# One ScalarE exponential over a two-bank PSUM tile for the first key tile of every head pair, with five single banks beside it

## The chip, the cores and the metric

The kernel runs on one core of a Trainium2 chip. The metric is the device time of one launch in microseconds (us); lower is better. Before the change the median of three runs is 174.76 us (173.38 to 174.87).

## The reference

Thresholded attention over 8 batches, 12 heads, 512 positions and 64 dimensions, in fp32:

```
scores  = einsum('bhqd,bhkd->bhqk', Q, K) / sqrt(64)
weights = softmax(scores)                      # over the keys
weights = where(weights > threshold, weights, 0)   # threshold 0.1
weights = weights / (sum(weights) + 1e-10)
out     = einsum('bhqk,bhkd->bhqd', weights, V)
```

Few weights of a softmax over 512 random scores pass 0.1, so most rows of the output are zero. The kernel uses that.

## The kernel before, in words

The 96 heads are taken as 48 pairs (hp), and two pairs make a quad (q, 24 of them). For each quad SyncE's queue loads Q and K. GpSimd casts Q to f16 (qcast, L371), TensorE transposes K in fp32 (ktr, L381) and Q in f16 (qtr, L410), ScalarE or VectorE copies the transposed K out of PSUM (kev, L389 and L391), VectorE the transposed Q (qev, L416), and GpSimd casts K to f16 (kh, L400). Squares of both for a bound on the norms (bits) are made by GpSimd (L425), VectorE (L429) or ScalarE (L427), and small matmuls (norms, L478) add them up.

Each pair has four key tiles t = 0 to 3. A step sc (L438) makes the scores of one key tile for both heads, two matmuls into two PSUM banks of 128 x 512 fp32. A step ex (L447 on ScalarE as a true exponential, L449 on VectorE as an approximation by the bits of an f16) reads one such bank and writes one half of an e tile. A step sm (L468) takes the e tile in four matmuls with a column of weights, and accumulates into one bank (sum) a row for each head, which later tells whether any query row of this pair can have a weight over the threshold. Three groups of 24, 16 and 8 pairs are closed one after the other (y, d, fl, mx), and for the few candidate rows the scores are computed again exactly (gq gathers the rows of Q, then xm, xev, xqk, xexp, xcut, xkeep), the row of V is gathered (gv) and scattered to the output (scatter), which 24 zero fills (z, L607) have blanked before.

PSUM has eight banks: seven in the pool `one`, one for `sum`. The pool `one` serves the scores, both transposes (two banks for each), the exact stage, the spare and warm-up matmuls, and one bank that the norms hold for most of the time.

What sets the order of all this is a table written out, ORDER: 1326 words, each of them a step's number in base 36 and a letter for the engine that does it (P TensorE, V VectorE, A ScalarE, G GpSimd, S and Q the DMA queues of SyncE and ScalarE, N none). The kernel issues the steps in that order, so every engine works through its own steps in the order of the table. A step that takes a buffer gets the one that came free first, and waits in place until it is free. The prices in `add(...)`, such as 0.478 us for an ex on ScalarE and 0.6 on VectorE, are those of the planner that such a table comes from; they do nothing at run time.

Of the kernel before, what the change touches and what calls it, by code (L numbers as in the profile page):

```python
# [9 lines left out]

ORDER = """6N fS 1G gS 7P hS 8P 5V 18S 24S 9P 22S aP 23S bP 16S 17Q 2vS iV jP 2tS nP kV lA cP mA oV 2uS dP pV 3qS qP yP rA sV eP 3pS zA 25V 10V 26P 19G uP 27A 12P 28V 3G wA 14V vA 1aP 29V 2aP 1bA 52S 2bV 1eP 1cA tP 2cV 13A xP 2wV 2dP 1fV 1dG 31P 1gV 2hP 2eA 32V 15P 1xG 2fV 2jA 2xP 33V 1tP 2yA 1pP 2zA 1vV 1uA 1hP 2iA 1jV 30G 2lP 1qA 11P 53S 2nV 3kG 3gP 1iA 2kP 6fS 1rV 1wP 2mA 38P 3iV 3hA 34P 36A 35V 3tP 3rG 3aA 1lP 3sG 3uV 3vA 37P 6gS 1nA 1mV 3yP 3wG 2pP 39A 7sS 3zV 3cP 2rA 40V 1sP 3lV 3dA 41P 2qV 56P 3mN 3xG 3eA 57A 58V 49P 2oP 4bA 54G 43V 45P 42A 3bP 55G 46V 4lP 47A 4tP 1yG 95S 4aV 4mA 44P 4dP 4vA 4nV 5bP 4uA 1kP 6jP 4eA 59G 5cV 5dV 1zN 2gP 6kA 6lV 5aG 5qP 4fV 5mP 5rA 6hG 5uP 1oP 5oA 5vV 6iG 7tS 5eP 5wA 5gV 6mG 96S 6oP 5fA 4oP 6pV 5sA aiS 5iP 6qV 4gP 5nA 5kV 7wP 5jA 6vP 7nV 7xA 4pP 7yV 6nG 4cP 6wA 5pP 6xV 6zP 7zG 4qA bvS 5yP 71V 70A 7oG 5tP 5hP 60A 4rV 7fP 99P 7gA 5zV 7jP 9aA 5xP 7kV 3jP 7hA 2sP 7uG 77P 9bA 66P 7vG 79V 78A 61P 5lP 9cG 67V 7lA 81P 7bP 9dG 68A 82V 7iP 6yP 7cA 97G 83V 6rP ajS 7dV 88P 98G 6tA 8cP bwS 89V 6sA 7mP 80G 3fP d8S 8aA 8eV 9eP 4xG 8dA amP 9fV 73P 9gV anA 7eP aoV 7pN 69P 74A a5P 8kP apG 75A a7V elS 62P a6A 4yG 4wP 8lV 84P 64A 7aP 86V 72P 85A 76P 8mA 63V 4hP 8gP 4iA 48P 4zN 8iV akG 9lP 8hA 9pP 4jV alG 9mA 8fP 87P 9rV 0G 9qA 8oP 8sP 9nA 8pV arP aqG 8tA 65P asV ioS a9P 8uA bxG atV a8P 8nP abA aaV byG auP 8qA 9hP 6aG avV b6P 9iA acP 8jP b7V 9jA 4kP b2P d9S awV b8A dcP b4A emS b3V a1P bqG ddA 8vP a3V k2S 9xP deA bzP a2V fzS 9zA ayP 9yV c0A fyS 9sP dfG biP azA c1V 8rP 8bP bkA bjV c4P c2G b0A 9tP 4sP c5V dgG 9vA 8wP 9uV baP c3G 8xA hcS a4P c6V axP bcA 8yV cfP epP chA bbV daG cbP eqA 9wP cgV dbG hbS b1P erA beP cdV 6bG 9oP bfA cjP bgV dhP ccA 9kP diV ckA czP clV cvP d0A bhP brG 6cN djV ciP cxA 8zP d1V ecP cwA dkP eeV bmP edA ceP b9P boA bnV bdP esG bsN dlA doP dmV crP enG dpA cmP dqV cnP eoG ctA e4P coV csA efP lfS etG 6uP blP e6A cpV g0G ipS euP e5A dsP adG evV e8P 21S dtA cyP ewV drP 3oS duA e9V g2P eaA exP g3V fdP g4A cqP feA cuP ezV g5G bpP eyA flP ffV g1G f5P fmA dnP fnV ebP aeG f7A k1S g7P f1P f6A g8V a0P e7P f3A g9V f9P f2A c7P fbV giP 2G afN c9A f0P foP 90V gkA dvP 51S faV fgP g6G gjA fhP c8V isP 91G fiA hfP fjV itA dwP iuA hgV f4P f8P dxA b5P dyV gqP k3G hhA 92N phS h2P gsV gaP grA k4G dzP gbA fcP gcV hdG d2P h3A fpP h4V heG geP fqA gdP ggV 4G gtP gfA gmP frV hkP goA guP leS hiG hlV ghP gvA fsP hmV glP iqG gnA gyP gwV hnP irG h0A e0P hpV gxP hjG hoA caP gzV gpP e2A ivG ixP i7P e1A iwG iyV hzP ekS i8A h5P izV lgG h1P i0V e3P i9A fkP lhG i1A j8P xtV hvP o4S j9A j4P 20P xuV j5A 6dP 7qP hxA btP xvN xwV 3nP agP j6A k5P xxV jaA jcP hwA o5S hqP xyV jdV jeA xzP msS 93P k6A 50P y0V ydV i3P mrS y1V k7A xrV y2G ibP i5A iaP i4V hyP idA ifP k8G icV joP ihA yeP ijG j7P yfV jfP igA jpV hrP 6eS ygV kaP htA jqV liP tlS hsA kbV jgP ljA h6V yhG huP kcV i2P jiA iiP lkV jhA jkP ikG khP jlV jsP kiA y3P jtV kjA klP egA y4V j0P knV k9G y5P ilN kmA h7V ehA juV h8N ysV j1V j2A ktP eiN llG piS yiP jmA kvV d3G tkS l1P yjA kpP y6A l3V ykP kqA y7V kuV krA mtG y8V l2A muG s7S lnP ylA kxP lmG loV mvP kyA ymV lpV d4G koP mwA ynV ksP l4P kzA meP mxV m2P mfA m6P mgV kkP m3A jnP s8S myG d5N m7V lyP m8A o8P jwG haS m0A m4V n0P lzA quS l0P n1V jbP o9A oaV kdP maP kfA n2V jrP o6G m5P mcV mbA n3P o7G n7P keA n5V mdP mzG m1P n8A qvS n4V nbP n9A mmG plP d7S ncV ndA ytP lqP fxS pmA pnV jvP n6P lrA nnP yuV lsV nvP noA pjG m9P yvV neP npV nwA obG l5P buS odP nxA l7V pkG miP l6A ieP oeV jxG luP mkA mjV ldS nqP j3P lvA ofV 7rS pqP lwA nrP yaV ogP 94S ntA mhP naP poG prV psV jyN ohA ltP oiV osP ocG nsA ptP ypV otV ooP ouA ywG l8P kgP oqV opA qyP puA pvV ppG q1P qzA uxS lxP s9G r0V pwP q2A p0P saG q3V owP p2A okP qwG oxV mlP oyA orP r1G p8P p1V omA sbP qxG olA paV qdP mqS ftG p9A ojP nuP scA sdV onP i6P qeV qfA q5P nfP uyS q6A q7V qlP yxP qnA seG nhV ngA r2G p4P yyV o3S r3P p5A p6V mnG pxP qmA p3P r4V kwP pzA q9P r5V pgS sgP qaA qbV qgP q8P pyA shV sfG riP moN njP yoV rjA rkV r6P nzG ovP nlA siV p7P nyP y9V r7A fuV ryP srP s0A yzP ssA ybG rzV r8A fvN stA nkV tmG jjP z0A tfV waS reP rqP tnG rgV toP rfA rsA yqG z1V r9P tpV nmP tqA q4P z2V t3P rrA rmP trG pbP t5A inS rnV o0G ttP roA rtP s6S z4V tuV ruP t4A qhP tvV wbS rvA qoP qiV ozP rwA twP uwS qjV t7P uzG o1N tyA k0S rpP t9V tsG u4P txA raP qtS usG u6A u5V rlP s1P rcA uoP t8V v1P rbA upV qcP uqA u8P z3V v2A v3V sjP ycG tjS q0P u9A rhP uaV ahS szP slA v0G weP skV t0A utG u0P wfV wgA niP qkP u1A rdP t1V rxP u2A snP z7V v6P soA ugP v4G v7V spA z8V ucP v5G uhA svP v8V z9N z5G ueA smP sxV sqP uiA vxP zaV v9P w9S swA t6P u3P vbA vaV wcG u7P udA w1P vyV wdG vtP vzA suP whG w2V ujP vuA ufP ubP s2G w3V vvA vpP wjP zbV vrA vdP taP vqA vfV tzP vwP veA wkV vlP wiG ukP vnA wlV vcP uuN s3G w0P umV ulA vhP wuP vmV vjA tbP t2P wvV wwA voP unP viA vsP tcV s4N wmP xmS tdA x2P zcV x6P wnA x3V vgP wxP woA urP x8V x4A wyP wqP x7V zdP wzA syP x5P zrV wsA vkP zeV x0V wrA xaP zgG xeP xcV xbA teP w4P xgA x1P xfV xdP wtP zfV x9P xiV xhP wpP zsP 106A ztV zhP w5V zvG 107V d6P ziA zjP 108N 109V 10aV 10bV tgV 10cP zkA zwP thN 10dV w6A 10fG h9P zxV zuV pcV zyP l9A w7N 10rV xjV z6G zlV xkN zmV znV zoV 10gP zzA zpG uvP 100V 10hA xlP qpV 101V 10iP yrG 102V laV pdV lbN peN zqG xnP 10jA xoP ejP qqA imP 10kV o2P 10lV tiP 104G mpP qrN xpP 10mV 10sV qsP 103V 10eV pfP 10nV fwP 10oG jzP xqP s5P w8P lcP 105G xsV 10qV 10tV 10pG"""


class Plan:
# [78 lines left out]
def kernel(  # L95
# [18 lines left out]
    nc = tc.nc  # L114
    B, H, S, D = Q.shape
    P = 128
# [26 lines left out]
    f32 = mybir.dt.float32  # L143
# [130 lines left out]
    nc.vector.memset(small[:], -SMALL)  # L274


    pools = {"one": 7, "sum": 1, "big": 32, "qh": 2, "e": 14,
             "y": 1, "vals": NG, "m": 2, "ix": NX, "qs": NX, "xq": 2, "cut": NX, "vr": NX}
    one = [psum.tile([P, S], f32, name=f"one{i}") for i in range(pools["one"])]
    sum_b = [psum.tile([P, S], f32, name=f"sum{i}") for i in range(pools["sum"])]  # L280

    def bufs(name, shape, dt):
# [33 lines left out]
    def at(pool, key):  # L316
        return plan.held[pool, key]
# [115 lines left out]
    def do_sc(eng, hp, t):  # L433
        q, n = divmod(hp, 2)
        qk = qk_b[big("qk", q)]
        for h in range(2):
            ps = slice(h * D, (h + 1) * D)
            nc.tensor.matmul(one[at("one", ("sc", hp, t, h))][:], lhsT=qk[ps, 1, n, t * P:(t + 1) * P], rhs=qk[ps, 0, n, :],  # L438
                             start=True, stop=True)

    kind = {}

    def do_ex(eng, hp, t, h):
        src = one[at("one", ("sc", hp, t, h))][:]
        dst = e_b[at("e", (hp, t))][:, h, :]
        if eng == "ACT":
            nc.scalar.activation(dst, src, ACTF.Exp, scale=scale, bias=-11.0 * math.log(2.0))  # L447
        else:
            nc.vector.tensor_scalar(dst.bitcast(u16), src, scale * LOG2E * 1024.0, 4096.0,  # L449
                                    op0=ALU.mult, op1=ALU.add)  # L450
        kind[hp, t, h] = 0 if eng == "ACT" else 1

    begun = set()

# [170 lines left out]
    for u in units:  # L625
# [39 lines left out]
        for hp in range(2 * q + n0, 2 * q + n0 + k):  # L665
            n = hp % 2
            for t in range(SO):
                g = 4 * hp + t
                add(("sc", hp, t), {"PE": 0.22}, 0.23, [("qev", u, 0), ("qev", u, 1), ("kh", q, n)], g - 3,
                    lambda e, hp=hp, t=t: do_sc(e, hp, t), takes=[("one", ("sc", hp, t, h)) for h in range(2)] + [("e", (hp, t))], mode="h")  # L670
                for h in range(2):
                    add(("ex", hp, t, h), {"ACT": 0.478, "DVE": 0.6}, 0.15, [("sc", hp, t)], g,
                        lambda e, hp=hp, t=t, h=h: do_ex(e, hp, t, h),
                        gives=[("one", ("sc", hp, t, h))])
                gr = group_of[hp]
                head = hp == first_of[gr] and t == 0
                add(("sm", hp, t), {"PE": 0.22}, 0.23,
                    [("ex", hp, t, 0), ("ex", hp, t, 1)] + ([("sm", first_of[gr], 0)] if not head else []), g + 2,
                    lambda e, hp=hp, t=t, gr=gr: do_sm(e, hp, t), takes=[("sum", gr)] if head else [],
                    gives=[("e", (hp, t))], mode="c")  # L680
        if not last:
# [172 lines left out]
```

## Time and profile before

| | |
|---|---|
| median of three runs | 174.76 us |
| the profiled execution | 173.97 us |
| its span, first to last instruction | 172.1 us |
| granted TensorE clock, mean | 0.992 |
| busy: PE, DVE, ACT, POOL | 159.3, 150.6, 146.7, 133.7 us |
| moved by DMA | 38.27 MB, mean 222 GB/s |

The profile is of one execution. The span is 1.9 us shorter than that execution's time, and that execution is 0.8 us below the median. Busy counts the union of an engine's instructions; instructions of one engine overlap at their ends, so the time from one start to the next is shorter than what one took. PE is matmul, PEld weight load, DVE VectorE, ACT ScalarE, POOL GpSimd, SP SyncE. L447 is line 447 of the kernel.

### The profile page before, as it was taken

Reading aid. Unit: us, or ns where it says so; the run is one execution under the profiler, and the core shown is the slowest. Engines: PE = TensorE matmul, PEld = TensorE weight load, DVE = VectorE, ACT = ScalarE, POOL = GpSimd, SP = SyncE. Lnnn points to the kernel's source line nnn. Section 1 sums busy time; section 2 is a strip of 40 time slices with the busy share of each in tenths; the row PEclk is TensorE's granted clock in tenths of the full one; section 3 lists DMA queues with packets and bytes.
Section 4 is the critical chain, followed back from the end, with each engine's and each line's share of the span. In section 5 each row is a group of like instructions: output and inputs, shape, how many; then the busy total and the mean of one; then the engine's idle time right before and its main releaser. Section 6 shows DMA issues by size and latency. Waiting matters only on the chain.

```text
span 172.1 us, 5805 instructions
## 1 busy us (share of the span) xinstructions
PE 159.3 (93%) x2190; PEld 62.5 (36%) x2190; DVE 150.6 (88%) x353; ACT 146.7 (85%) x294; POOL 133.7 (78%) x201
## 2 busy tenths in 40 slices
PE   5699999999999999999989999989999999999940
PEld 1253544342444234334432443434324333432410
DVE  5398999899999989989999899999999999989630
ACT  2279999999999999999899999999999999746300
POOL 5049794999988979993796999999899985226762
PEclk9999999999999999999999999999999999999996
DMA  4999998959899999878999996999999980000000
GB/s 103 290 281 175 268 255 224 265 132 313 183 244 304 277 229 339 242 181 251 276 280 289 221 272 156 365 409 311 318 304 338 415 344 13 2 3 8 3 3 9
DMA packets 67453, 38.27 MB, mean 222 GB/s; under 512 B 51941, under 2 KB 64349, under 8 KB 67424
## 3 DMA queue, kind: packets, MB, share of 16 engines
q1 hardware_dynamic: 66320, 37.63, 77.7%
q8 instruction: 17, 0.28, 0.7%
q0 software_dynamic: 576, 0.13, 0.5%
q10 hardware_dynamic: 528, 0.13, 0.3%
q14 instruction: 12, 0.10, 0.3%
HBM read 25.56 MB, written 12.78 MB: 223 GB/s over the span
## 4 chain that ended last, share of the span: by engine, by line
PE 55%; DMA 15%; DVE 10%; POOL 6%; ACT 4%; issue 4%; SPq 2%; POOLq 0%; DVEq 0%
PE one L438 20%; PE sum L468 19%; DMA qs<-in_Q_dram,idx 7%; PE one L556 6%; PE one L381 4%; PE one L410 3%; ACT e L447 3%; DMA out_dram<-zero 3%; POOL big L425 2%; DMA big<-in_K_dram 2%; DVE e L449 2%; DMA big<-in_Q_dram 2%; POOL qh L371 2%; PE one L541 2%; SPq L330 2%
## 5 line engine op out<-in xcount | busy, mean ns | idle before, releaser
L447 ACT ACTIVATE e<-one 128x512 f16<-128x512 f32 x238 | 123.3, 638 | 3.0 <-PE one L438 2.5
L449 DVE TENSOR_SCALAR e<-one 128x512 uint16<-128x512 f32 x146 | 93.5, 682 | 4.2 <-PE one L438 3.4
L438 PE MATMUL one<-big 64*128 64x512 f16 x384 | 66.4, 385 | 0.3
L468 PE MATMUL sum<-e,w_s 128*32 128x512 f16 (+1 forms) x768 | 58.4, 385 | 0.3 <-DVE y L495 0.2
L425 POOL TENSOR_TENSOR big<-big 128x512 bf16<-128x512 f16 x56 | 56.9, 1037 | 0.0
L400 POOL CAST big<-big 128x512 f16<-128x512 f32 x46 | 27.6, 611 | 8.6 <-DVE big L429 3.3
L371 POOL CAST qh<-big 128x512 f16<-128x512 f32 x45 | 26.5, 612 | 7.9 <-DVE qh L369 6.3
L438 PEld LDWEIGHTS <-big 64*128 64x128 f16 x384 | 17.1, 95 | 36.5 <-issue 28.0
L468 PEld LDWEIGHTS <-w_s 128*32 128x32 f16 (+1 forms) x768 | 15.3, 95 | 31.6 <-issue 27.0
L389 ACT COPY big<-one 128x512 f32<-128x512 f32 (+1 forms) x33 | 18.5, 591 | 3.8 <-PE one L381 3.8
L416 DVE COPY big<-one 128x512 f16<-128x512 f16 (+1 forms) x52 | 19.2, 396 | 1.2 <-PE one L410 0.7
L381 PE MATMUL one<-identity_f,big 64*128 64x64 f32 x384 | 18.1, 231 | 1.6 <-DMA big<-in_K_dram 1.4
L381 PEld LDWEIGHTS one<-identity_f,big 64*128 64x128 f32 x384 | 16.5, 143 | 6.4 <-issue 2.7
L534 POOL DMA_INDIRECT qs<-in_Q_dram,idx x6 | 6.4, 1072 | 12.5 <-DVE idx L524 12.2
L391 DVE COPY big<-one 128x512 f32<-128x512 f32 (+1 forms) x19 | 12.5, 657 | 1.3 <-PE one L381 0.6
L556 PE MATMUL one<-big,xq 128*32 128x512 f32 x96 | 11.5, 598 | 0.4 <-DVE xq L549 0.2
L410 PE MATMUL one<-identity_h,qh 64*128 64x64 f16 x384 | 10.8, 193 | 0.7 <-DVE qh L369 0.4
L410 PEld LDWEIGHTS <-qh 64*128 64x128 f16 x384 | 8.7, 96 | 7.2 <-issue 3.1
L600 POOL DMA_INDIRECT out_dram<-vr,idx x6 | 6.4, 1065 | 2.6 <-issue 1.1
L585 POOL DMA_INDIRECT vr<-in_V_dram,idx x6 | 6.4, 1060 | 2.3 <-DVE cut L566 1.2
L562 ACT ACTIVATE one<-one 128x512 f32<-128x512 f32 x6 | 3.5, 584 | 5.4 <-PE one L556 5.3
L429 DVE TENSOR_SCALAR big<-big 128x512 int32<-128x512 int32 x15 | 7.3, 491 | 0.1
(85 smaller groups left out, 80.8 us busy)
## 6 DMA issues: line engine op xcount, KB each, us to landing
out_dram<-zero SPq DMA_DIRECT2D x24, 512.0 KB, 6.9
big<-in_K_dram SPq DMA_DIRECT2D x95, 128.0 KB, 4.7
big<-in_Q_dram SPq DMA_DIRECT2D x22, 512.0 KB, 5.7
big<-in_Q_dram SPq DMA_DIRECT2D x4, 256.0 KB, 3.8
big<-in_K_dram ACTq DMA_DIRECT2D x1, 128.0 KB, 2.8
qs<-in_Q_dram,idx POOLq DMA_INDIRECT x6, 3.4
vr<-in_V_dram,idx POOLq DMA_INDIRECT x6, 2.4
out_dram<-vr,idx POOLq DMA_INDIRECT x6, 2.2
```

The source lines that it names most:

```text
L371: behind(nc.gpsimd.tensor_copy(dst, src))
L381: nc.tensor.matmul(dst[i][:, c:c + D], lhsT=src[ps, n0 + n, r, :], rhs=identity_f32[ps, ps], is_transpose=True, start=True, stop=True)
L389: nc.scalar.copy(dst, src)
L400: behind(nc.gpsimd.tensor_copy(dst, src))
L410: nc.tensor.matmul(dst[i][:, c:c + D], lhsT=src[ps, n0 + n, r, :], rhs=identity_h[ps, ps], is_transpose=True, start=True, stop=True)
L416: nc.vector.tensor_copy(qk_b[big("qk", q)][:, 0, n0:n0 + k, i * SO * D:(i + 1) * SO * D], src)
L425: behind(nc.gpsimd.tensor_tensor(out=dst[:, n, :], in0=src[:, n, :], in1=src[:, n, :], op=ALU.mult))
L438: nc.tensor.matmul(one[at("one", ("sc", hp, t, h))][:], lhsT=qk[ps, 1, n, t * P:(t + 1) * P], rhs=qk[ps, 0, n, :], start=True, stop=True)
L447: nc.scalar.activation(dst, src, ACTF.Exp, scale=scale, bias=-11.0 * math.log(2.0))
L449: nc.vector.tensor_scalar(dst.bitcast(u16), src, scale * LOG2E * 1024.0, 4096.0, op0=ALU.mult, op1=ALU.add)
L468: nc.tensor.matmul(dst[32 * j:32 * j + 32, :], lhsT=w, rhs=x, start=first, stop=False, skip_group_check=True)
L556: nc.tensor.matmul(one[at("one", ("xs", x))][sl, :], lhsT=xq_b[at("xq", x)][:, n, sl], rhs=kt_b[big("kt", quads[j])][:, n, :], start=(n == ...
```

## The change

The first key tile (t = 0) of every pair gets a PSUM tile of its own of two banks, `two`, of which there is one. Its two score matmuls write the two halves, and one instruction on ScalarE takes the exponential of all 1024 columns. The pool `one` shrinks from seven banks to five. The 96 steps ex of the first key tiles become 48, all on ScalarE, so the table has 1278 words. The whole table is another one: other engines for many steps, and another order on every engine and on SyncE's queue.

```diff
-ORDER = """6N fS 1G gS 7P hS 8P 5V 18S 24S 9P 22S aP 23S bP ...
+ORDER = """6N 1G fQ gS hQ 17S 7P 20S 8P 0G 5V 15S 16S 9P 3G ...
...
-    pools = {"one": 7, "sum": 1, "big": 32, "qh": 2, "e": 14,
+    pools = {"one": 5, "two": 1, "sum": 1, "big": 32, "qh": 2, "e": 14,
...
+    two = [psum.tile([P, 2, S], f32, name=f"two{i}") for i in range(pools["two"])]
...
-            nc.tensor.matmul(one[at("one", ("sc", hp, t, h))][:], lhsT=qk[ps, 1, n, t * P:(t + 1) * P], rhs=qk[ps, 0, n, :],
+            dst = one[at("one", ("sc", hp, t, h))][:] if t else two[at("two", ("sc", hp))][:, h, :]
+            nc.tensor.matmul(dst, lhsT=qk[ps, 1, n, t * P:(t + 1) * P], rhs=qk[ps, 0, n, :],
                              start=True, stop=True)
...
     def do_ex(eng, hp, t, h):
-        src = one[at("one", ("sc", hp, t, h))][:]
-        dst = e_b[at("e", (hp, t))][:, h, :]
+        if t:
+            src, dst = one[at("one", ("sc", hp, t, h))][:], e_b[at("e", (hp, t))][:, h, :]
+        else:
+            src = two[at("two", ("sc", hp))][:].rearrange("p h s -> p (h s)")
+            dst = e_b[at("e", (hp, t))][:].rearrange("p h s -> p (h s)")
         if eng == "ACT":
             nc.scalar.activation(dst, src, ACTF.Exp, scale=scale, bias=-11.0 * math.log(2.0))
...
-                for h in range(2):
-                    add(("ex", hp, t, h), {"ACT": 0.478, "DVE": 0.6}, 0.15, [("sc", hp, t)], g,
+                for h in range(2 if t else 1):
+                    add(("ex", hp, t, h), {"ACT": 0.478, "DVE": 0.6} if t else {"ACT": 0.845}, 0.15, [("sc", hp, t)], g,
                         lambda e, hp=hp, t=t, h=h: do_ex(e, hp, t, h),
-                        gives=[("one", ("sc", hp, t, h))])
+                        gives=[("one", ("sc", hp, t, h)) if t else ("two", ("sc", hp))])
```

Read step by step, the two tables differ so in who does what (steps, before and after):

| step | ScalarE | VectorE | GpSimd |
|---|---|---|---|
| ex, 512 columns | 238, 154 | 146, 134 | |
| ex, 1024 columns | 0, 48 | | |
| kev, two pairs (512 columns) | 27, 20 | 17, 24 | |
| kev, one pair (256 columns) | 6, 5 | 2, 3 | |
| bits | 5, 3 | 15, 21 | 28, 24 |
| y, xev | 1 and 3, 3 and 4 | 2 and 3, 0 and 2 | |
| qcast, kh | 0 and 1, 1 and 2 | 3 and 1, 1 and 1 | 45 and 46, 46 and 45 |

TensorE's steps are the same 490, in another order. In the order before, the kind of tiling changes from one step to the next (rows of 64 for sc, ktr, qtr; columns of 32 for sm, norms; whole) 208 times, in the order after 219 times. At the start, the first load of Q goes to ScalarE's queue behind one K load, where SyncE's queue had it third. On SyncE's queue 12 zero fills instead of 7 come after the last load of Q. At the end, no bits step stands between y and d of the last group on VectorE.

## Rows read from the trace of the kernel before

**Rows 1.** The page: busy time by engine, and the chain that ended last.
```profile
PE 159.3 (93%) x2190; PEld 62.5 (36%) x2190; DVE 150.6 (88%) x353; ACT 146.7 (85%) x294; POOL 133.7 (78%) x201
PE 55%; DMA 15%; DVE 10%; POOL 6%; ACT 4%; issue 4%; SPq 2%; POOLq 0%; DVEq 0%
```

**Rows 2.** Windows: length, busy time (instructions) of PE, PEld, DVE, ACT, POOL; clock, DMA share, GB/s.
```profile
8.00:150.00 142.00, 139.96 (x2004) 55.88 (x2004) 134.89 (x266) 138.09 (x279) 120.68 (x181) 1.00 0.92 258
...
130.00:150.50 20.50, 20.25 (x277) 7.68 (x275) 19.64 (x38) 19.01 (x38) 14.48 (x18) 1.00 0.57 216
```

**Rows 3.** The chain in order of time, TensorE's steps: start us, us, what.
```profile
39.83 0.35 PE one L438 x2
...
40.94 0.54 PE one L438 x4
...
49.35 0.33 PE sum L468 x4
50.00 0.55 PE sum L468 x8
50.55 0.34 PE one L410 x16
...
52.86 0.49 PE one L381 x16
...
93.43 1.85 PE one L556 x16
```

**Rows 4.** Timeline of ScalarE: start us, us, line, operation, tiles, count, idle before.
```profile
11.38 0.66 ACT L389 COPY big<-one 128x256 f32<-128x256 f32 x2
11.89 0.64 ACT L447 ACTIVATE e<-one 128x512 f16<-128x512 f32 x1
...
38.47 9.42 ACT L447 ACTIVATE e<-one 128x512 f16<-128x512 f32 x19
47.62 1.25 ACT L389 COPY big<-one 128x512 f32<-128x512 f32 x2
48.56 0.80 ACT L447 ACTIVATE e<-one 128x512 f16<-128x512 f32 x1
...
154.41 1.99 ACT L427 ACTIVATE big<-big 128x1024 bf16<-128x1024 f16 x2
```

**Rows 5.** Groups by line and form: count, busy us, mean ns of one, idle before.
```profile
L447 ACT ACTIVATE e<-one 128x512 f16<-128x512 f32 x238 | 123.3, 638 | 3.0 <-PE one L438 2.5
L449 DVE TENSOR_SCALAR e<-one 128x512 uint16<-128x512 f32 x146 | 93.5, 682 | 4.2 <-PE one L438 3.4
...
L427 ACT ACTIVATE big<-big 128x1024 bf16<-128x1024 f16 x5 | 5.2, 1053 | 0.0
...
L425 POOL TENSOR_TENSOR big<-big 128x512 bf16<-128x512 f16 x56 | 56.9, 1037 | 0.0
...
L429 DVE TENSOR_SCALAR big<-big 128x512 int32<-128x512 int32 x15 | 7.3, 491 | 0.1
```

**Rows 6.** Timeline of VectorE: start us, us, line, operation, tiles, count.
```profile
35.66 1.88 DVE L449 TENSOR_SCALAR e<-one 128x512 uint16<-128x512 f32 x3
37.46 0.74 DVE L416 COPY big<-one 128x512 f16<-128x512 f16 x2
38.14 0.69 DVE L391 COPY big<-one 128x512 f32<-128x512 f32 x1
```

**Rows 7.** Waits, longest first: engine and line, waited for, us, times, longest.
```profile
PEld one L381 <- ACT e L447: 2.2, 7, 0.4
```

**Rows 8.** The chain at the start and at the end: start us, us, what.
```profile
2.40 3.50 DMA big<-in_Q_dram
...
6.80 0.98 PE one L340 x8
7.78 0.96 PE one L438 x3
...
151.04 0.33 DVE big L429
```

More of the change, by code (lines that the diff above doesn't have):

```diff
@@ L450, in do_ex @@
                                     op0=ALU.mult, op1=ALU.add)
-        kind[hp, t, h] = 0 if eng == "ACT" else 1
+        for i in (0, 1) if t == 0 else (h,):
+            kind[hp, t, i] = 0 if eng == "ACT" else 1
     begun = set()
@@ L669 @@
                 add(("sc", hp, t), {"PE": 0.22}, 0.23, [("qev", u, 0), ("qev", u, 1), ("kh", q, n)], g - 3,
-                    lambda e, hp=hp, t=t: do_sc(e, hp, t), takes=[("one", ("sc", hp, t, h)) for h in range(2)] + [("e", (hp, t))], mode="h")
-                for h in range(2):
-                    add(("ex", hp, t, h), {"ACT": 0.478, "DVE": 0.6}, 0.15, [("sc", hp, t)], g,
+                    lambda e, hp=hp, t=t: do_sc(e, hp, t), takes=([("one", ("sc", hp, t, h)) for h in range(2)] if t else [("two", ("sc", hp))]) + [("e", (hp, t))], mode="h")
+                for h in range(2 if t else 1):
+                    add(("ex", hp, t, h), {"ACT": 0.478, "DVE": 0.6} if t else {"ACT": 0.845}, 0.15, [("sc", hp, t)], g,
                         lambda e, hp=hp, t=t, h=h: do_ex(e, hp, t, h),
-                        gives=[("one", ("sc", hp, t, h))])
+                        gives=[("one", ("sc", hp, t, h)) if t else ("two", ("sc", hp))])
                 gr = group_of[hp]
@@ L677 @@
                 add(("sm", hp, t), {"PE": 0.22}, 0.23,
-                    [("ex", hp, t, 0), ("ex", hp, t, 1)] + ([("sm", first_of[gr], 0)] if not head else []), g + 2,
+                    [("ex", hp, t, h) for h in range(2 if t else 1)] + ([("sm", first_of[gr], 0)] if not head else []), g + 2,
                     lambda e, hp=hp, t=t, gr=gr: do_sm(e, hp, t), takes=[("sum", gr)] if head else [],
```

2 lines of the change are left out of this document (1 added, 1 removed).

## The prediction

> **What bounds the kernel now.** I read the page first. TensorE leads with 93% of the span busy, VectorE and ScalarE follow with 88 and 85%, and the chain that ended last lies 55% on TensorE, 10% on VectorE and only 4% on ScalarE [rows 1]. Next the windows. Between 8 and 150 us, where the scores, exponentials and sums run, the three engines are busy for 140.0, 134.9 and 138.1 of 142 us [rows 2]. Busy time flatters them all, since neighbours overlap, so each engine has to be priced from start to start.
>
> For TensorE I take the chain in order of time. One sm step on its own is 0.33 us and two in a row are 0.55, so a further step costs 0.215 and the first after another kind of tiling about 0.115 more; the scores go the same way (0.35 and 0.54); a Q transpose is 0.34, a K transpose 0.49, an exact stage's product 1.85 [rows 3]. Over the middle that makes 384 x 0.215 = 82.6 for sc and sm, 24 x (0.34 + 0.49) = 19.9 for the transposes, three products 5.6, eight norms 1.7, and 197 of the 208 changes of kind fall there, 22.7. Together 132.5 of 142 us, 93%.
>
> For ScalarE, 19 exponentials of 512 columns start within 9.15 us, 0.482 each [rows 4]. With 238 of them 114.7, 27 copies of 512 columns and 6 of 256 at 0.47 and 0.255 (below) 14.2, and some 4 for the rest, it is near 133 of 142, or 94%. On VectorE three exponentials start within 1.80 us, 0.60 each, and a Q copy is 0.34 [rows 6]; 146 and 52 of them make 105, and the K copies, bits and small steps some 20 more, about 88%.
>
> So nothing is far from full, and TensorE works to the pace at which banks come free: the exponentials still waited 2.5 + 3.4 us for scores [rows 5], and the transposes 2.2 us for exponentials that held their banks [rows 7]. DMA moves the same bytes in both kernels and is 92% busy in the middle, but only 57% at its end [rows 2], so I take it for no bound within a few us.
>
> **The price of the wide exponential.** No row shows an exponential of 1024 columns. Two copies of 256 columns start 0.255 us apart, two of 512 columns 0.47 [rows 4]: 0.84 ns for a column. Added to 0.482 that gives 0.482 + 512 x 0.00084 = 0.91 us. The only instruction of 1024 columns, a square out of SBUF, has 1.99 us for two of which the last took 1.05, hence 0.94 from start to start [rows 4, 5]. The diff's own price is 0.845. I take 0.91, since it is from PSUM as here, and keep 0.845 below and 0.964 (two halves, nothing saved) above. The gain on a pair is then 0.05 us, where the new table was laid out for 0.11.
>
> The Trainium skill's page "ScalarE: Activation LUTs", in What ACT_TABLE_LOAD costs, has one element per cycle at 1.2 GHz, 0.833 ns a column, whatever the function. By that page 1024 columns stream for 0.853 us with no fixed part, so 0.845 could not be reached, and 0.482 + 0.427 would be 0.909; the trace's 0.84 ns agrees.
>
> **Part by part.** *ScalarE:* 84 single exponentials go, 84 x 0.482 = -40.5; 48 wide ones come, +43.7; kev -7 x 0.47 - 0.255 = -3.5; two bits -1.9; two y, one xev, one qcast, one kh, at up to 0.482 each, +2.2. Sum 0.0 (at 0.845 it is -3.1, at 0.964 +2.6). *VectorE:* 12 exponentials -7.2; seven kev of 512 columns at 0.60 and a narrow one, +4.5; six bits at 0.49 [rows 5], +2.9; y, xev and qcast by the nearest rows (0.60, 0.34) -2.2. Sum -2.0. So what the change takes from ScalarE, the new table spends on copies of which VectorE was to be relieved too; the pair of engines has 2.0 us less to do, 1.0 each if perfectly shared. *GpSimd:* four bits of two instructions at 1.04 us [rows 5], -8.3; it is not the bound, I count nothing.
>
> *TensorE:* the same 490 steps, but 11 more changes of kind, 11 x 0.115 = +1.3 us, on the engine that holds most of the chain. That the sequence is cut more finely is what fewer banks would do: fewer scores can be made in a row.
>
> *Banks:* a score bank is held for a write of 0.35 [rows 3] and an exponential of 0.64 or 0.68 [rows 5], 1.0 us at least. A pair lasts 142 / 48 = 2.96 us and has ten uses of single banks (eight halves of scores, and two for the quad's transposes). With the norms holding one, six banks give each use 1.78 us, 0.78 to spare. After, eight uses share four banks, 1.48 us, 0.48 to spare. The one double tile is held some 1.3 us of 2.96 and then lies empty; it can take nothing else. The waits that this slack absorbs, 5.9 + 2.2 = 8.1 us now, I scale by 0.78 / 0.48 = 1.6: +4.9 us over three engines side by side, a third of it on the path, +1.6. Against it the relief of 1.0. Net +0.6; ends -2.0 and +5. Queued behind a late double tile are, on TensorE, the sums and transposes of other pairs, and on ScalarE, which alone can empty it, single exponentials.
>
> *Start:* the first Q load is issued at 2.40 us and lands 3.50 later [rows 8]; behind a single K load it may be issued about 1.0 sooner, -1.0. But three warm-up steps instead of two now stand between the first Q transpose and the first scores, and two took 0.98 [rows 8], so +0.49. I take -0.5; ends -1.0 and +0.5. *End:* a bits step of 0.33 us leaves the chain between y and d [rows 8], -0.3. *SyncE's queue:* five more zero fills behind the last Q load bring it earlier, and the fills have the close of the last group to finish beside; nothing counted, some 1 us if the last gathers have to wait for them.
>
> Sum: 1.3 + 0.6 - 0.5 - 0.3 = +1.1. The profiled execution took 173.97 us (span 172.1 and 1.9 around it), which makes 175.1 for its like; it stands 0.8 below the median of 174.76, so against the runs shown **175.9 us**. With the ends of the terms this case holds 174.0 to 177.4. About 1%, 1.75 us, is what a measurement of this kernel can tell from no change, so this is no change by a narrow margin.
>
> **The rivals.** *The exponentials bound, and the banks suffice.* Then TensorE's 1.3 us disappear in its waits. With 0.91 the two engines win 1.0 and start and end 0.8: -1.8, 173.0. With 0.845 they win 5.1 / 2 = 2.6: -3.4, 171.4. For it: ScalarE's 94% in the middle is as high as TensorE's. Against it: ScalarE has 4% of the chain [rows 1], and its own sum falls by nothing at the price that the rows give. I put it at 172.2, chance 0.29.
>
> *The transposes starve the exponentials.* A transpose takes two of the four single banks at once for 1.0 us or more. In that time one tile of scores is left, which both engines together clear in about 0.54 us (0.482 and 0.60), and the next can't be written: 0.48 us lost on both, unless the double tile falls just there. There are 25 transposes of K and 25 of Q in the middle. Two of 50 uncovered beyond the waits that I scaled decide for slower by over 1%; five give +2.4 on top of my 1.1, 178.3; ten +4.8, 180.7. For it: the waits of transposes for exponentials that show already [rows 7], and the finer cut of TensorE's order. Against it: the new order was laid out for five banks, and each double tile comes once in 2.96 us, nearly as often as a transpose. Chance 0.26, at 178.3.
>
> *The wide instruction saves nothing*, as two banks read in one go cost what two halves do, 0.964. Then ScalarE has 2.6 us more to do than I counted, half of which lands on the path: 177.2. For it: the square's 0.94. Chance 0.07.
>
> **How the numbers follow.** My case has 0.38, the rivals 0.29, 0.26 and 0.07. Faster by over 1% (below 173.0): nearly all of the first rival and a sliver of mine, 0.29. Slower by over 1% (above 176.5): most of the second and third and the upper end of mine, 0.35. Within 1%: 0.36. The range reaches from just below the first rival's better end, 171.2, to between five and ten uncovered transposes, 179.8; about one in eight falls outside.
>
> **What would show it.** Right: the 48 wide instructions start 0.91 us apart when they follow one another or another exponential; TensorE's busy share unchanged with sm and sc in shorter runs; more waits of L438 and of both transposes for exponentials; the first scores about 0.5 us earlier than 7.78 [rows 8]; the chain still mostly TensorE. Wrong: ScalarE's sum clearly lower and the last exponential ending 2 us or more earlier, which would say that the exponentials set the pace; or gaps on ScalarE and VectorE just behind transposes, of half a us each and more than a few, which is the second rival. A wide instruction at 0.85 would overturn the price that I rest most on.

## The result, and the profile after

The changed kernel takes 176.94 us (174.93 to 177.02, four runs) against 174.81 us for the kernel before on the same occasion: a ratio of 1.0106, 95% interval 1.0058 to 1.0154, so some 1.9 us slower. The ratio, here and below, is taken over executions in the faster of two states that the chip shows, so it is not the quotient of the medians. The profiled executions stand 177.02 to 173.97 us, spans 175.2 to 172.1; the first is the slowest of its four, so the traces differ by more than the ratio, 3.1 us.

The page of the changed kernel first, the lines that answer to [rows 1] and to the ScalarE and VectorE groups of [rows 5]:

```profile
PE 162.9 (93%) x2190; PEld 63.0 (36%) x2190; DVE 148.2 (85%) x350; ACT 148.5 (85%) x253; POOL 126.2 (72%) x193
PE 76%; DVE 6%; ACT 6%; DMA 4%; issue 3%; POOL 3%; ACTq 0%; POOLq 0%; DVEq 0%
L454 DVE TENSOR_SCALAR e<-one 128x512 uint16<-128x512 f32 x134 | 87.2, 685 | 6.3 <-PE one L440 5.0
L452 ACT ACTIVATE e<-one 128x512 f16<-128x512 f32 x154 | 85.3, 611 | 4.2 <-PE one L440 3.6
L452 ACT ACTIVATE e<-two 128x1024 f16<-128x1024 f32 x48 | 50.1, 1043 | 0.0
```

VectorE does 2.4 us less than before, ScalarE 1.8 us more, GpSimd 7.5 us less. No engine is nearer to full than it was, and yet the exponentials' idle time for scores has grown on both engines, from 2.5 and 3.4 us [rows 5] to 3.6 and 5.0. The wide exponential itself never stood idle.

I cut both traces at two points, the start of the first scores and the end of the last sum.

| us | first scores | middle | last sum ends | from there to the end of the span |
|---|---|---|---|---|
| before | 7.71 | 142.8 | 150.47 | 21.6 |
| after | 7.98 | 147.5 | 155.48 | 19.7 |

So the middle lost 4.7 us, the end won 1.9 and the start lost 0.3. Single profiles scatter here: in three kernels whose steps are the same up to the last sum (before, before_tail and before_gv below) the middle reads 142.8, 144.0 and 142.7, so a difference of about 1 us between two middles says little. By window, from 8 to 150 us, the changed kernel shows, against [rows 2]:

```profile
8.00:150.00 142.00, 139.30 (x1936) 53.83 (x1932) 130.19 (x258) 135.68 (x230) 109.42 (x165) 1.00 0.92 257
...
70.00:110.00 40.00, 38.40 (x536) 14.77 (x532) 35.25 (x78) 36.58 (x65) 26.66 (x44) 1.00 0.83 240
```

The second row is the stretch in which the first group of pairs is closed: VectorE is busy for 35.25 of 40 us and ScalarE for 36.58, where the kernel before has 37.91 and 38.87. There the middle loses most: of the 192 steps of scores, counted in the order of time, the 97th starts at 75.2 us before and 77.2 after, the 121st at 97.5 and 102.8, the 145th at 114.8 and 119.2. TensorE's timeline in that stretch (start us, us, line, operation, tiles, count, idle before and who ended it):

```profile
86.13 0.39 PE L440 MATMUL one<-big 64*128 64x512 f16 x1
86.73 0.37 PE L440 MATMUL one<-big 64*128 64x512 f16 x1 [0.22 <-ACT big L390]
...
89.38 0.39 PE L440 MATMUL one<-big 64*128 64x512 f16 x1
89.97 0.37 PE L440 MATMUL one<-big 64*128 64x512 f16 x1 [0.20 <-DVE big L417]
...
92.56 0.65 PE L547 MATMUL one<-mask_x,qs 128*64 128x256 f32 x4 [0.88 <-ACT e L452]
```

Twice the two halves of one step of scores are torn apart, because the bank for the second half was still being read by a copy; and the exact stage's L547 stood 0.88 us in front of everything else on TensorE for a bank that an exponential held. ScalarE's timeline beside it shows what that costs (same columns):

```profile
87.64 1.02 ACT L452 ACTIVATE e<-two 128x1024 f16<-128x1024 f32 x1
88.54 1.09 ACT L452 ACTIVATE e<-one 128x512 f16<-128x512 f32 x2
90.38 0.60 ACT L452 ACTIVATE e<-one 128x512 f16<-128x512 f32 x1 [0.74 <-PE one L440]
91.44 1.08 ACT L452 ACTIVATE e<-one 128x512 f16<-128x512 f32 x2 [0.46 <-PE one L440]
93.25 0.37 ACT L553 COPY xq<-one 128x256 f32<-128x256 f32 x1 [0.73 <-PE one L547]
93.52 1.03 ACT L452 ACTIVATE e<-two 128x1024 f16<-128x1024 f32 x1
94.44 1.09 ACT L452 ACTIVATE e<-one 128x512 f16<-128x512 f32 x2
```

Three gaps within 3.6 us, 1.93 us together. The same rows carry the price of the wide exponential: from 87.64 to 88.54 and from 93.52 to 94.44 are 0.90 and 0.92 us from start to start. Over the 39 of 48 that another exponential follows without a gap the median is 0.905 us (shortest 0.904); over 117 of the narrow ones it is 0.478.

At the start the chain reads (start us, us, what), against [rows 8]:

```profile
1.45 4.30 DMA big<-in_Q_dram
...
5.77 0.44 DVE qh L370
...
6.64 1.40 PE one L341 x9
8.05 0.54 PE one L440 x2
```

Q's first load is issued 0.95 us sooner, but takes 4.30 us instead of 3.50 and so lands 0.15 us sooner; the warm-up steps take 0.42 us more.

At the end, the last exact exponential (ScalarE, L562 before, L568 after) and the gathers and scatters of V on GpSimd decide. Before, ScalarE and GpSimd:

```profile
160.56 0.58 ACT L562 ACTIVATE one<-one 128x512 f32<-128x512 f32 x1 [2.04 <-PE one L556]
```

```profile
161.69 1.01 POOL L600 DMA_INDIRECT out_dram<-vr,idx  x1 [0.57 <-DVE cut L566]
163.00 1.05 POOL L585 DMA_INDIRECT vr<-in_V_dram,idx  x1 [0.30 <-DVE ix L529]
164.36 1.02 POOL L585 DMA_INDIRECT vr<-in_V_dram,idx  x1 [0.31 <-issue]
```

After, likewise:

```profile
165.29 0.58 ACT L568 ACTIVATE one<-one 128x512 f32<-128x512 f32 x1 [2.04 <-PE one L562]
```

```profile
165.09 1.02 POOL L606 DMA_INDIRECT out_dram<-vr,idx  x1 [0.30 <-issue]
167.54 1.04 POOL L591 DMA_INDIRECT vr<-in_V_dram,idx  x1 [1.43 <-DVE idx L586]
```

Before, a scatter and another gather stood in GpSimd's queue ahead of the last gather, which came 3.80 us behind the exponential. In the new order they are through, and the last gather comes 2.25 us behind it. That is 1.55 of the 1.9 us; up to the exponential the end is 0.28 us shorter (9.81 us from the last sum, 10.09 before), and behind the gather it is the same.

### The profile page after: what moved, and what is told of

It is laid out like the page before. It is cut to its first block, busy times and chain, and to the rows that moved or that the text cites. A ratio compares the mean times of both kernels' runs of the same rounds, so it can differ in the third digit from the quotient of the medians.

```text
span 175.2 us, 5747 instructions
## 1 busy us (share of the span) xinstructions
PE 162.9 (93%) x2190; PEld 63.0 (36%) x2190; DVE 148.2 (85%) x350; ACT 148.5 (85%) x253; POOL 126.2 (72%) x193
## 4 chain that ended last, share of the span: by engine, by line
PE 76%; DVE 6%; ACT 6%; DMA 4%; issue 3%; POOL 3%; ACTq 0%; POOLq 0%; DVEq 0%
PE sum L474 25%; PE one L440 22%; PE one L382 8%; PE two L440 6%; ACT e L452 5%; PE one L562 4%; PE one L411 4%; DVE e L454 4%; PE one L484 3%; DMA big<-in_Q_dram 2%; PE one L547 1%; DMA qs<-in_Q_dram,idx 1%; POOL out_dram L606 1%; POOL big L426 1%; ACT big L390 1%
## 5 line engine op out<-in xcount | busy, mean ns | idle before, releaser
L454 DVE TENSOR_SCALAR e<-one 128x512 uint16<-128x512 f32 x134 | 87.2, 685 | 6.3 <-PE one L440 5.0
L452 ACT ACTIVATE e<-one 128x512 f16<-128x512 f32 x154 | 85.3, 611 | 4.2 <-PE one L440 3.6
L474 PE MATMUL sum<-e,w_s 128*32 128x512 f16 (+1 forms) x768 | 59.9, 387 | 0.0
L440 PE MATMUL one<-big 64*128 64x512 f16 x288 | 58.4, 390 | 0.5 <-ACT big L390 0.2
L426 POOL TENSOR_TENSOR big<-big 128x512 bf16<-128x512 f16 x48 | 48.9, 1040 | 3.9 <-DVE big L417 1.6
L452 ACT ACTIVATE e<-two 128x1024 f16<-128x1024 f32 x48 | 50.1, 1043 | 0.0
L372 POOL CAST qh<-big 128x512 f16<-128x512 f32 x46 | 27.4, 614 | 16.9 <-DVE big L399 3.6
L440 PE MATMUL two<-big 64*128 64x512 f16 x96 | 19.7, 388 | 0.3 <-DVE big L417 0.2
L392 DVE COPY big<-one 128x512 f32<-128x512 f32 (+1 forms) x27 | 17.3, 657 | 3.0 <-PE one L382 1.5
L390 ACT COPY big<-one 128x512 f32<-128x512 f32 (+1 forms) x25 | 13.3, 556 | 2.5 <-PE one L382 2.0
L562 PE MATMUL one<-big,xq 128*32 128x512 f32 x96 | 11.5, 598 | 0.3 <-ACT xq L553 0.2
L568 ACT ACTIVATE one<-one 128x512 f32<-128x512 f32 x6 | 3.5, 582 | 6.4 <-PE one L562 6.3
```

The lines of the kernel that those rows point to most:

```text
L372: behind(nc.gpsimd.tensor_copy(dst, src))
L392: nc.vector.tensor_copy(dst, src)
L426: behind(nc.gpsimd.tensor_tensor(out=dst[:, n, :], in0=src[:, n, :], in1=src[:, n, :], op=ALU.mult))
L440: nc.tensor.matmul(dst, lhsT=qk[ps, 1, n, t * P:(t + 1) * P], rhs=qk[ps, 0, n, :], start=True, stop=True)
L474: nc.tensor.matmul(dst[32 * j:32 * j + 32, :], lhsT=w, rhs=x, start=first, stop=False, skip_group_check=True)
L562: nc.tensor.matmul(one[at("one", ("xs", x))][sl, :], lhsT=xq_b[at("xq", x)][:, n, sl], rhs=kt_b[big("kt", quads[j])][:, n, :], start=(n == ...
```

## The experiments

All were timed beside the kernel before; the first four rows of the table ran together, so did the next four and the next three, the last by itself, and ratios from different groups compare less sharply than those of one. The changed kernel itself was timed in none of these groups: its 1.0106 is that of the result, and its middle there 147.5 us. The theory after the result: the middle's loss comes from ScalarE, since the wide exponential takes 0.905 us where the order was laid out for 0.845, and from fewer single banks. Its rival: the new sequence of steps is slower as such, whatever the price and the banks. Middle and end are those of one profile each; after_dve has none that compares.

| kernel | ratio to before, 95% interval | middle, us | end, us |
|---|---|---|---|
| after_split | 1.0212 [1.0159, 1.0266] | 150.1 | 19.8 |
| after_seven | 1.0109 [1.0038, 1.0180] | 148.1 | 19.8 |
| before_six | 1.0867 [1.0807, 1.0927] | 159.4 | 22.2 |
| before_tail | 1.0081 [1.0015, 1.0148] | 144.0 | 23.3 |
| after_short | 1.0006 [0.9973, 1.0040] | 145.6 | 19.8 |
| after_dve | 1.0052 [1.0010, 1.0093] | | |
| before_act | 1.0004 [0.9965, 1.0044] | 143.8 | 21.7 |
| before_gv | 1.0108 [1.0058, 1.0159] | 142.7 | 23.0 |
| after_seven_short | 0.9956 [0.9902, 1.0010] | 145.7 | 19.7 |
| before_pe | 0.9993 [0.9938, 1.0048] | 144.7 | 21.8 |
| after_pe | 0.9970 [0.9927, 1.0014] | 146.0 | 19.8 |
| before_pe_zero | 0.9968 [0.9926, 1.0009] | 143.1 | 21.6 |

**after_split**: the changed kernel, each wide exponential as two of 512 columns.

```diff
-            nc.scalar.activation(dst, src, ACTF.Exp, ...)
+            for c in range(0, 2 * S, S) if t == 0 else (None,):
+                sl = slice(None) if c is None else slice(c, c + S)
+                nc.scalar.activation(dst[:, sl], src[:, sl], ACTF.Exp, ...)
```

> The kernel after, each wide exponential split into two of 512 columns on ScalarE; banks, order and everything else as after. 48 pairs lose 2 x 0.478 - 0.904 = 0.05 us each, 2.5 us of ScalarE's work. If ScalarE is off the path (bank theory: TensorE waits for banks that both exponential engines hold), the time rises by 0 to 1.2 us over the kernel after, to 177 to 178. If the exponential engines set the pace, it rises by the full 2.5, to 179.5.

Measured: 1.0212, a hundredth or 1.85 us more than the change itself, for 48 x (0.956 - 0.905) = 2.4 us more on ScalarE; the middle is 2.6 us longer. In this order, most of what the exponentials of the first key tiles cost goes into the middle, and the single instruction is worth about 2 us.

**after_seven**: besides, the seven single banks given back, in the same order.

```diff
-    pools = {"one": 5, "two": 1, "sum": 1, ...
+    pools = {"one": 7, "sum": 1, ...
...
-            dst = one[at("one", ("sc", hp, t, h))][:] if t else two[at("two", ("sc", hp))][:, h, :]
+            dst = one[at("one", ("sc", hp, t, h))][:]
```

> The kernel after with seven single banks again: the scores of the first key tile go to two of them, and ScalarE takes their exponentials in two instructions of 512 columns, one behind the other. Order and engines as after. Bank theory (the 4.8 us that the middle lost are waits for banks): most of it comes back, 3 to 4 us less than with the split instruction alone, so 174 to 175, at or below the kernel before, since the end of the order after is 1.9 us shorter. Order theory (the order itself, laid out for a wide exponential at 0.845 and with more changes of tiling, is the slower one): no better than the split instruction alone, 177 to 179.

Measured: 1.0109. Beside after_split, with the same instructions on the same occasion, the two banks give back 1.0%, or 2.0 us of the middle; the two intervals overlap a little, so the size is uncertain. With the banks and the 512-column instructions of before, the new order still has a middle of 148.1 us.

**before_six**: the kernel before with one bank fewer, its order untouched.

```diff
-    pools = {"one": 7, "sum": 1, ...
+    pools = {"one": 6, "sum": 1, ...
```

> The kernel before with six single banks instead of seven, all else as before; its order never needs the seventh to go on. Bank theory: the spare time of a use falls from 0.78 to about 0.48 us as in the kernel after, and the middle gets 3 to 5 us longer, 178 to 180. Order theory: 0 to 1 us longer, 175 to 176.

Measured: 1.0867, far over what was expected. Groups and window of that kernel:

```profile
L447 ACT ACTIVATE e<-one 128x512 f16<-128x512 f32 x238 | 125.8, 605 | 9.9 <-PE one L438 8.2 <-PE sum L468 0.2
```

```profile
8.00:150.00 142.00, 136.42 (x1803) 51.49 (x1800) 121.39 (x236) 128.15 (x251) 111.04 (x169) 1.00 0.89 243
```

ScalarE's wait for scores goes from 2.5 [rows 5] to 8.2 us, and in the 142 us all three engines lose at once, VectorE most (134.9 to 121.4). A step that has to wait holds every later step of its engine, which is how I read this: an order is good for its number of banks. The changed kernel, with five, is far from such a loss, so its order had to be another one; the two banks that after_seven gives back to it are worth 1.0%.

**before_tail**: the kernel before with four steps moved in the order, to see whether GpSimd's queue explains the shorter end.

```diff
-... ztV zhP w5V zvG ... 101V 10iP yrG 102V ... 10lV tiP 104G mpP ... 10nV fwP 10oG jzP ...
+... ztV zhP zvG ... 10aV 10bV w5V ... 10gP zzA yrG zpG ... 102V 104G laV ... 10mV 10oG 10sV ...
```

> The kernel before with four steps moved in its order after the last scores: the scatter of stage 1 ahead of the gather of V of stage 3, the gathers of V of stages 4 and 5 right behind the steps that make their indices, and one bits step of VectorE behind the candidates of the last group. In the trace before, GpSimd issues the gather of stage 4 at 163.0 us though its index was ready at 159.6, and that of stage 5 1.4 us behind it. If the shorter end of the kernel after (19.7 us from the last sum to the end of the span, 21.6 before) comes from this queue's order, the time falls by 1.5 to 2.3 us, to 172.5 to 173.3; if it comes from elsewhere, by less than 0.5.

Measured: 1.0081, a loss where a gain was expected. The link itself shortened as expected: the last gather comes 2.26 us behind the exact exponential. But that exponential came late. ScalarE, then TensorE, of that kernel ("remote" is a wait for which the profile names nobody):

```profile
164.75 0.58 ACT L562 ACTIVATE one<-one 128x512 f32<-128x512 f32 x1 [4.74 <-remote]
```

```profile
160.06 1.92 PE L556 MATMUL one<-big,xq 128*32 128x512 f32 x16 [0.43 <-issue]
```

The product that it reads ends at 161.98 in the trace, and the exponential starts 2.77 us later, with nothing else before it on ScalarE. Before, the product ends at about 160.5 and the exponential starts at 160.56 us.

**before_gv**: the same without the move of the bits step w5V, that is with the three GpSimd steps moved alone.

> The kernel before with three steps moved on GpSimd's queue after the last scores: the scatter of stage 1 ahead of the gather of V of stage 3, the gathers of V of stages 4 and 5 right behind the steps that make their indices; unlike the run with the shortened end before, no bits step is moved. If that run lost what the queue gave because the last product's signal came 2.7 us after its modelled end by accident of that run, this one is 1.0 to 2.0 us faster than the kernel before, ratio 0.988 to 0.994. If such a delay belongs to any order with these moves, no faster.

Measured: 1.0108, and the same picture, a last sum at 150.55 us as before and an exponential that starts at 163.65 behind a product that ended at 160.90. So the late signal goes with the moved gathers and scatters, in both kernels that have them; in none of the other profiles does this exponential start more than 0.7 us behind its product. Why they delay it, no run here tells; that GpSimd's order made the changed kernel's end shorter is read from its trace and not confirmed by a timed gain.

**after_short**: the changed kernel, each wide exponential cut to 952 of 1024 columns once its buffer has been filled (the other 72 columns of weights are left as an earlier pair had them).

```diff
-            nc.scalar.activation(dst, src, ACTF.Exp, ...)
+            c = S if t else 2 * S - 72 * (at("e", (hp, t)) in full)
+            nc.scalar.activation(dst[:, 0:c], src[:, 0:c], ACTF.Exp, ...)
```

> The kernel after, with the wide exponentials cut to 952 of 1024 columns (the last 72 columns of the second head keep what an earlier pair left in that buffer), where the buffer has been filled once. 72 x 0.833 ns = 0.06 us off each of some 44, so that one costs the 0.845 us that the order was laid out for: 2.6 us less for ScalarE and nothing else changed. If ScalarE sets the pace of this order (splitting the wide instruction added 2.5 us to ScalarE and 2.6 us to the time), the time falls by 1.5 to 2.6 us against the kernel after, to a ratio of about 1.00 with the kernel before. If TensorE and its banks set it, by less than 0.8 us, ratio 1.006 or more.

Measured: 1.0006. (The 2.6 us that the expectation quotes are the middle's; by the ratio it was 1.85.) The cut instruction goes from start to start in 0.845 us, which is the price in the table of steps, and with it the changed kernel is level with the one before. The 0.06 us, taken off 44 of the 48, are 2.6 us on ScalarE and brought 1.0%, 1.75 us. Level only in sum: the middle, 145.6 us, is still 2.8 longer than before, and the end 1.8 shorter.

**after_dve**: the changed kernel, VectorE's exponentials cut to 492 columns, 2.6 us off VectorE.

```diff
+            c = S - 20 * (at("e", (hp, t)) in full)
-            nc.vector.tensor_scalar(dst.bitcast(u16), src, ...
+            nc.vector.tensor_scalar(dst[:, 0:c].bitcast(u16), src[:, 0:c], ...
```

> The kernel after, with VectorE's exponentials cut to 492 of 512 columns (the rest keeps what an earlier pair left), where the buffer has been filled once: 20 columns at 0.96 GHz are 0.021 us each, 2.6 us in all off VectorE, nothing else changed. If ScalarE alone sets the pace of this order, less than 0.8 us comes off, ratio 1.006 or more. If both exponential engines do, because a score bank that either holds keeps TensorE waiting, 1.5 us or more, ratio about 1.00.

Measured: 1.0052, half a per cent under the change, about 0.9 us for 2.6 taken away, but the two intervals overlap. If VectorE counts, it counts less than the wide exponentials; that it doesn't is not excluded.

**before_act**: the kernel before, ScalarE's exponentials cut to 498 columns, 2.6 us off ScalarE.

```diff
+            c = S - 14 * (at("e", (hp, t)) in full)
-            nc.scalar.activation(dst, src, ACTF.Exp, ...)
+            nc.scalar.activation(dst[:, 0:c], src[:, 0:c], ACTF.Exp, ...)
```

> The kernel before, with ScalarE's exponentials cut to 498 of 512 columns (the rest keeps what an earlier pair left), where the buffer has been filled once: 0.0117 us off each of some 220, 2.6 us off ScalarE, nothing else changed. If TensorE sets the pace before the change, as the prediction said, the time falls by less than 0.8 us, ratio 0.995 or more. If the exponentials set it, as the first rival said, by 1.5 us or more, ratio 0.991 or less.

Measured: 1.0004. Before, quicker exponentials on ScalarE alone save nothing: the interval excludes the 0.991 of a kernel that they pace.

**after_seven_short**: after_seven, with the two halves of each first key tile cut to 447 columns, so that banks and price are what the order could wish for.

```diff
-                nc.scalar.activation(e_b[...][:, i, :], one[...][:], ACTF.Exp, ...)
+                c = S - 65 * (t == 0 and at("e", (hp, t)) in full)
+                nc.scalar.activation(e_b[...][:, i, 0:c], one[...][:, 0:c], ACTF.Exp, ...)
```

> The changed kernel's order with seven single banks again, and each first key tile's exponential as two ScalarE instructions of 447 of the 512 columns (the other 65 columns of each half are left out and keep what an earlier pair left). By the 512-column row that is about 0.84 to 0.85 us of ScalarE per pair, the price for which the order was laid out. So nothing of the change is left but its order. Theory A (the middle's loss is the dearer instruction plus the missing bank, and the order itself costs nothing at the price it was made for): the middle, first scores to last sum, is about 145.6 - 2.0 = 143.6 us, beside 142.8 before; with the end 1.9 us shorter the ratio is 0.988 to 0.994. Theory B (the sequence itself is slower, whatever the price and the banks): the middle stays at 145 us or above and the ratio at 0.997 or more.

Measured: 0.9956, between the two, and the interval reaches into both. The middle, 145.7 us, speaks for the rival: even so it is longer than before's, and only the shorter end brings the total down. How much the sequence alone costs stays open, between nothing and 3 us. Beside after_short, this kernel also says that the two parts of the theory do not add up: with the exponential at 0.845, the banks given back leave the middle where it was (145.6 and 145.7 us) and the ratios differ by 0.5%, with overlapping intervals. So price and banks together explain 1.8 of the 4.7 us that the middle lost, or 2.6 us by the ratios (1.0106 and 0.9956), not 2 us each.

**before_pe** and **after_pe**: the kernel before, and the changed one, with 56 of 512 columns left out of two of a pair's four sums, 96 steps in all and 2.3 us off TensorE.

```diff
+        a, b = (56, S) if t == 1 and not first else (0, S - 56) if t == 2 and not first else (0, S)
...
-            nc.tensor.matmul(dst[32 * j:32 * j + 32, :], ...
+            nc.tensor.matmul(dst[32 * j:32 * j + 32, a:b], ...
```

> The kernel before, with less work for TensorE alone: the sums of key tiles 1 and 2 leave out 56 of their 512 columns each (not in a group's first pair), 96 instructions in all. By the row of a 512-column sum, 0.215 us, that is 96 x 0.0235 = 2.3 us off TensorE and nothing off the exponential engines. Theory A (as predicted: TensorE sets the pace before): 1.5 to 2.2 us less, ratio 0.987 to 0.992. Theory B (the pace before is shared, TensorE waits for banks somewhere else as soon as it is quicker): under 0.5 us, ratio 0.997 or more.

> The changed kernel with the same 96 sums cut by 56 columns, 2.3 us off TensorE alone. Theory A (ScalarE and the banks have taken the pace over from TensorE): under 0.8 us less, ratio to the kernel before 1.006 or more. Theory B (TensorE still sets the pace, slowed by the changes of kind): 1.5 to 2.2 us less, ratio 1.002 or below.

Measured: 0.9993 and 0.9970. In the changed kernel TensorE's time counts after all: 1.4% less than the change by the ratios, 1.5 us by the middles of the profiles, so theory A of that run falls; TensorE gives back about as much there as the wide exponentials do. In the kernel before, it does not count: the interval excludes the 0.987 to 0.992 of a kernel that TensorE paces. The groups of before_pe show that the cut was made, and its waits (engine and line, waited for, us, times, longest) where some of it went:

```profile
L469 PE MATMUL sum<-e,w_s 128*32 128x512 f16 x192 | 33.5, 384 | 0.2 <-DVE y L496 0.2
...
L469 PE MATMUL sum<-e,w_s 128*32 128x456 f16 x192 | 31.1, 361 | 0.1
```

```profile
POOL qh L371 <- DMA big<-in_Q_dram: 4.8, 5, 1.8
PEld L410 <- POOL qh L371: 4.3, 10, 0.9
```

Q's transposes wait for GpSimd's casts, and those for the loads of Q.

**before_pe_zero**: so, the same with the zero fills cut to one eighth.

```diff
-        inst = issuer(eng).dma_start(out=Oz[q], in_=zero[:])
+        inst = issuer(eng).dma_start(out=Oz[q][0:16], in_=zero[0:16])
```

> The kernel before with the 96 shorter sums of the earlier cut (2.3 us off TensorE), and besides with the zero fills of the output reduced to one eighth of their rows (the other rows of the output are left unfilled): 24 transfers of 64 KB in place of 512 KB, 11 of the 38 MB that the kernel moves. The earlier cut alone left the time where it was, and in its trace GpSimd's casts waited 4.8 us for Q's loads and TensorE 8.2 us for GpSimd (before: 0.6 and 4.9). Theory A (the kernel before is held by two things at once: as soon as TensorE is quicker, the stream of loads is late): without the fills the loads come sooner, TensorE's 2.3 us show, ratio 0.985 to 0.992. Theory B (the loads are no bound; the order of the steps gives the time back elsewhere): ratio 0.996 or more.

Measured: 0.9968. The window shows the traffic gone and the engines where they were:

```profile
8.00:150.00 142.00, 139.06 (x1996) 56.14 (x1998) 134.56 (x264) 137.71 (x279) 120.66 (x181) 1.00 0.75 181
```

DMA falls from 92% to 75% busy, the loads of Q now keep GpSimd waiting for 1.2 us instead of 4.8, and still TensorE's 2.3 us do not show. So it was not the late loads that kept them from showing.

## Why the prediction was right, and where not

The forecast was +1.1 us, no change by a narrow margin, with 0.35 for slower by over 1%. It came out about 1.9 us slower by the ratio, 1.06%, just over that line; the two profiled executions differ by 3.1. The time is inside the range, the sign of the forecast was right, and its size too small. That it came so near is partly luck: the waits were forecast 3.2 us too small, and an end 1.6 us shorter than forecast, for a reason that I had not seen, took half of that back. By terms:

**The price of the wide exponential** was right: 0.91 taken, 0.905 measured. The working was right too: (0.905 - 0.478) / 512 is 0.834 ns a column, as the two copies of [rows 4] had it. The Trainium skill's page "ScalarE: Activation LUTs", in What ACT_TABLE_LOAD costs, has 0.833 ns; the trace agrees. The third rival, that two banks in one go save nothing, is thereby excluded: 0.905 against 2 x 0.478 = 0.956, and after_split has a difference of about 1% of the kernel's time for it.

**ScalarE's and VectorE's sums** were nearly right, 0.0 and -2.0 us forecast, +1.8 and -2.4 on the page. The *relief* of 1.0 us that I drew from them was the wrong use of them. I took the two engines as a pair that shares its gain. In the changed order two thirds to three quarters of what is added to the wide exponentials or taken from them shows in the time (1.85 of 2.4 us in after_split, 1.75 of 2.6 in after_short), of VectorE's about a third, if any (after_dve), and ScalarE won nothing. The pace is not ScalarE's alone either, as most of TensorE's 2.3 us came back too (after_pe). At the planned 0.845 the change would have been level (after_short), so the first rival's 171.4 for that price was out of reach as well: the price alone is worth 1.75 us.

**What bounds the kernel before.** I wrote that TensorE works to the pace at which banks come free and took the pace to be TensorE's. That failed: 2.3 us off TensorE change nothing (before_pe), nor do 2.6 us off ScalarE (before_act). No single one of the two holds that kernel; with either quicker, the time goes into waits for the other or for its suppliers. VectorE and GpSimd were not cut there, so whether one of them holds it alone is open. The 55% of the chain on TensorE [rows 1] did not say what TensorE's time is worth.

**TensorE's +1.3** for more changes of kind was about right as a sum of work. Thirteen more of them fall in the middle, and a warm-up step falls out of it. With every step of both traces priced at the tenth percentile of its kind's times from start to start (kinds told apart by size and by whether a change of tiling follows), the middle of TensorE sums to 129.1 us before and 130.1 after. The rest of the middle, in which TensorE waits, goes from some 13.6 to 17.3 us. So most of the loss is in waits.

**Banks and waits**, +0.6 forecast, is the term that was mis-sized: about +3.8 us in the profiles. What I left out is that the order relies on 0.845: 2.9 us more on ScalarE than it was laid out for. I had seen that the gain on a pair was half the planned one, and put it down as a smaller gain; it is a delay for every step that the table put behind it. What is left of the middle's loss without the dearer price and the missing banks, 2.9 us by the profile of after_seven_short and about 1 by its ratio, lies with the sequence or with nothing, and stays open.

Of the steps within the term, the banks' own +1.6 stands near the 2.0 us between after_split and after_seven, but by luck, since its count was wrong. The norms do not hold a bank for most of the time, as the words on the kernel before have it and the prediction took over. They take it with their first step and give it back when the maximum over it (L491) is taken. In the kernel before, the windows of the norms' line alone (stretch, length, busy time of PE and PEld with their instructions, clock, DMA share, GB/s), and L491 on VectorE:

```profile
8.00:78.00 70.00, 0.00 (x0) 0.00 (x0) 1.00 0.97 244
78.00:84.00 6.00, 2.10 (x32) 0.67 (x32) 1.00 0.96 250
84.00:150.00 66.00, 0.00 (x0) 0.00 (x0) 1.00 0.86 273
```

```profile
82.89 0.68 DVE L491 TENSOR_REDUCE nmax<-one 128x1 f32<-128x512 f32 x1
```

From 78.9 to 83.6 us is 5 of the 142. So seven banks serve ten uses before and five serve eight after, 1.07 and 0.85 us to spare by the same working, and the same scaling would have given +0.7. Besides, before_six, in which that slack falls from 1.07 to 0.78 us, lost 15 us: the mean slack does not tell what a bank is worth under a given order.

The middle also loses 3.3 us in the one stretch, 77 to 103 us, where the exact stage and the transposes, and up to 85.6 us the norms, need single banks at once; the second rival spoke of transposes only, and gaps of half a us behind each of them are not what the trace shows.

**The start**, -0.5 forecast, was +0.3. The earlier issue, 0.95 us, was as forecast, but the load took 0.80 us longer and ate it. The warm-up's +0.49 was +0.42, but I had not taken off that the same step leaves the middle.

**The end**, -0.3 forecast, was -1.9. The bits step was the least of it: up to the last exponential the end won 0.28 us. I had counted SyncE's queue past the last gathers but not GpSimd's own, in which the last gather stood behind a scatter and a gather of another stage (3.80 us against 2.25 behind the same exponential).

## What to carry to other kernels

When a written-out order is built on an instruction price, compare that price with a pitch worked out from the trace first: where the instruction is on the path, most of the difference times the count comes back as delay, as some 1.75 of 2.6 us did here. Price a buffer taken away by the order that has to live with it: one PSUM bank fewer cost 15 us under an order laid out for seven, while the two set aside here, under an order laid out for that, cost some 2 us in one pair of runs (after_split, after_seven) and nothing to be seen in another (after_short, after_seven_short). And neither a busy share of 93% nor 55% of the chain shows that an engine's time can be had back; cutting a few columns of its instructions does, and here it paid in one kernel and not in the other.

## What the runs showed of the hardware

One exponential over two PSUM banks starts 0.905 us before the next, two over one bank each 0.956; the saving, 0.05 us, is what one such instruction takes beyond its 512 x 0.834 ns. Cut to 952 columns it is 0.845. On TensorE, a matmul of the sums took 0.361 us with 456 columns and 0.384 with 512. With three GpSimd steps moved, an exponential on ScalarE began 2.75 us after the end that the profile gives for the product that it reads (2.77 with a fourth step moved); the cause is open.
